# Expert dispatch: weights loaded in 1 KB runs on the ScalarE queue and put in tile order by VectorE block transposes

## The chip, the cores and the metric

The kernel runs on one core of a Trainium2 chip. The metric is the device time of one execution in microseconds (us). A profile of one execution shows what each engine and each DMA queue did; its span is a little shorter than the time, since the time also holds what lies around the program.

## What is computed

Each of 16 x 1024 tokens has a row of 512 floats and k = 2 weights, one for each of its experts. The output holds each token's row twice, each copy scaled by one weight:

```python
x_expanded = x[:, :, np.newaxis, :].repeat(k, axis=2)
weights = expert_weights[..., np.newaxis]
return (x_expanded * weights).astype(np.float32)
```

The expert indices are not used. 33.6 MB of x are read, 131 KB of weights, and 67.1 MB are written.

## The kernel before

The 16,384 tokens are cut into 8 tiles of 2,048 tokens. Partition p of a tile holds 16 consecutive tokens, so a tile of x is 128 partitions by 8,192 floats (4 MB), and each partition's part is one run of 32 KB in HBM. The weights lie in one SBUF tile of 128 x 256 floats, `w_tile`; column `c = i * 32 + t * 2 + kk` of partition p is weight kk of token t of that partition in tile i. A column of `w_tile` is thus the per-partition scalar of one multiply.

In HBM the 32 weights that a partition needs for one tile are one run of 128 B, and the runs of its 8 tiles lie 16 KB apart. L54 and L55 load them with eight DMAs on SyncE's queue, one for each tile: each has 128 rows of 128 B, 16 KB. They are issued at the start, ahead of all output.

Loads of x are issued by ScalarE (L76), one DMA per tile, into a pool of two buffers. The first two are issued at the start (L79 and L80); load i + 2 is issued at the end of tile i's loop (L109), and waits until both engines are done with the tile that had its buffer.

For each of the 16 tokens t of a tile there are two multiplies of 128 x 512: VectorE makes the copy for kk = 0 (L97, TENSOR_SCALAR) and ScalarE that for kk = 1 (L91, ACTIVATE). Eight tokens fill one `o_tile` (128 x 8,192 floats, 4 MB), of which there are four buffers. SyncE writes it to HBM (L105), so there are 16 writes, two for each tile. The multiplies of a half tile wait for its x tile, for the weights of its columns, and for an `o_tile` buffer to be written out.

[...] The scheduler places semaphore waits by region: a multiply waits for the DMA that wrote its columns of `w_tile`. It has eight semaphores for DMAs and gives them out in turn. With eight weight DMAs ahead, the second load of x got the semaphore of the first weight DMA and waits for it to land, and the eighth weight DMA got that of the first load of x and waits for that. ScalarE also loads its table of functions once (ACT_TABLE_LOAD) ahead of its first multiply.

Of the kernel before, what the change touches and what calls it, by code (L numbers as in the profile page):

```python
# [1 line left out]

# [4 lines left out]


@with_exitstack
def kernel(  # L10
    ctx: ExitStack,
    tc: tile.TileContext,
    x: bass.AP,
    expert_indices: bass.AP,
    expert_weights: bass.AP,
    out: bass.AP,
):
    nc = tc.nc

    batch, seq, hidden = x.shape  # L20
    k = expert_weights.shape[-1]
    P = nc.NUM_PARTITIONS
    ntok = batch * seq
    assert ntok % P == 0
    A_TOTAL = ntok // P

    f32 = mybir.dt.float32
    row = k * hidden
    TX = 16
    TO = 8  # L30


    groups = [[16], [16], [16], [16], [16], [16], [16], [16]]
    assert sum(sum(g) for g in groups) == A_TOTAL

    xf = x.rearrange("b s h -> (b s) h")
    of = out.rearrange("b s k h -> (b s) (k h)")
    wf = expert_weights.rearrange("b s k -> (b s) k")

    w_pool = ctx.enter_context(tc.tile_pool(name="w_pool", bufs=1))  # L40
    x_pool = ctx.enter_context(tc.tile_pool(name="x_pool", bufs=2))
    o_pool = ctx.enter_context(tc.tile_pool(name="o_pool", bufs=4))

    w_tile = w_pool.tile([P, A_TOTAL * k], f32)

    def rows(of_all, done, T):
        return of_all[done * P : (done + T) * P, :].rearrange(
            "(p a) n -> p (a n)", a=T
        )

    weights = []
    for group in groups:
        weights.append((sum(n for _, n in weights), sum(group)))
    for at, T in weights:  # L54
        nc.sync.dma_start(out=w_tile[:, at * k : (at + T) * k], in_=rows(wf, at, T))  # L55

    tiles = []
    done = 0
    for group in groups:
        T = sum(group)  # L60
        a0 = 0
        for n in group:
            tiles.append((done, T, a0, n))
            a0 += n
        done += T

    loaded = []

    def load(i):
        if i >= len(tiles):  # L70
            return
        done, T, a0, n = tiles[i]
        x_tile = x_pool.tile([P, TX * hidden], f32)
        cols = rows(xf, done, T)[:, a0 * hidden : (a0 + n) * hidden]
        for lo, hi in [(0, P)]:
            nc.scalar.dma_start(out=x_tile[lo:hi, : n * hidden], in_=cols[lo:hi, :])  # L76
        loaded.append(x_tile)

    for i in range(2):  # L79
        load(i)  # L80
    for i, (done, T, a0, n) in enumerate(tiles):
        x_tile = loaded[i]
        outr = rows(of, done, T)
        for t in range(n):
            if t % TO == 0:
                o_tile = o_pool.tile([P, TO * row], f32)
            for kk in range(k):
                c = (done + a0 + t) * k + kk
                o = t % TO * row + kk * hidden
                if kk == 1:  # L90
                    nc.scalar.mul(  # L91
                        out=o_tile[:, o : o + hidden],
                        in_=x_tile[:, t * hidden : (t + 1) * hidden],
                        mul=w_tile[:, c : c + 1],
                    )
                    continue
                nc.vector.tensor_scalar(  # L97
                    out=o_tile[:, o : o + hidden],
                    in0=x_tile[:, t * hidden : (t + 1) * hidden],
                    scalar1=w_tile[:, c : c + 1],  # L100
                    scalar2=None,
                    op0=mybir.AluOpType.mult,
                )
            if (t + 1) % TO == 0:
                nc.sync.dma_start(  # L105
                    out=outr[:, (a0 + t + 1 - TO) * row : (a0 + t + 1) * row],
                    in_=o_tile,
                )
        load(i + 2)  # L109

# [1 line left out]
_INS = ['x', 'expert_indices', 'expert_weights']  # L112
_OUTS = [((16, 1024, 2, 512), 'float32')]


# [23 lines left out]
```

## Time and profile before

| | |
|---|---|
| time, median of 3 runs | 240.91 us (240.27 to 241.28) |
| time of the profiled execution | 240.2 us |
| TENSOR_SCALAR 128 x 512, VectorE | 128 of them, mean 480 ns |
| ACTIVATE 128 x 512, ScalarE | 128 of them, mean 708 ns |
| VectorE, ScalarE busy | 51.9 us, 81.3 us |
| HBM read, written | 33.69 MB, 67.11 MB |
| rate over 0 to 10, 10 to 20, 20 to 24 us | 346, 441, 286 GB/s |
| rate over 24 to 28, 28 to 228, 228 to 238 us | 402, 433, 357 GB/s |
| issue to landing, median: x, weights, output | 23.2, 21.1, 48.3 us |

The rates come from the view of stretches, which counts a packet's bytes where it starts. The two engines that compute are idle most of the time, and what ended most of their idle time is the landing of writes (`out_dram<-o_tile`: 115.6 us of VectorE's idle time, 96.1 us of ScalarE's). A DMA's landing is when its last byte is reported; the time from issue to landing holds the time it queued.

### The profile page before, as it was taken

The page shows a single profiled execution, that of the slowest core. Times are in us where ns is not written, and L with a number is a line of the kernel's source. Part 1 is how long each engine was busy: PE and PEld are TensorE (multiplying, and loading weights), DVE is VectorE, ACT ScalarE, POOL GpSimd, SP SyncE. Part 2 cuts the span into 40 slices and gives each one's busy share as a digit, 9 for nine tenths or more (in the row PEclk, how much of TensorE's full clock was granted, in tenths as well). Part 3 has the DMA queues.
Part 4 walks back from the last instruction along what each step waited for, and adds up shares of the span by engine and source line. Part 5 has one row for each costly group of instructions (what it writes and reads, how often), then busy time and mean ns, then how long its engine had stood idle before and what let it go on. Part 6 is the DMA issues. An engine that isn't in the chain of part 4 may idle for free.

```text
span 238.4 us, 384 instructions
## 1 busy us (share of the span) xinstructions
DVE 51.9 (22%) x128; ACT 81.3 (34%) x129; POOL 0.2 (0%) x4
## 2 busy tenths in 40 slices
DVE  0072910055005004050230503204040235000000
ACT  0278970086207007080260803417043256200000
POOL 0000000000000000000000000000000000000000
DMA  7999999999999999999999999999999999999996
GB/s 266 441 442 357 441 429 412 423 429 429 440 440 440 437 434 434 440 440 418 423 429 423 434 440 440 434 440 434 440 429 440 434 429 412 429 429 440 440 440 264
DMA packets 4610, 100.81 MB, mean 423 GB/s; under 512 B 1536, under 2 KB 1536, under 8 KB 1536
## 3 DMA queue, kind: packets, MB, share of 16 engines
q1 hardware_dynamic: 3456, 67.24, 65.6%
q10 hardware_dynamic: 1152, 33.55, 33.2%
q14 instruction: 2, 0.02, 0.0%
HBM read 33.69 MB, written 67.11 MB: 423 GB/s over the span
## 4 chain that ended last, share of the span: by engine, by line
DMA 60%; another core or an unknown queue 12%; ACT 12%; ACTq 1%; issue 0%
DMA out_dram<-o_tile 41%; DMA x_tile<-in_x_dram 16%; ACT o_tile L91 12%; DMA w_tile<-in_expert_weights_dram 3%; ACTq L76 0%; ACTq L134 0%; ACTq L91 0%
## 5 line engine op out<-in xcount | busy, mean ns | idle before, releaser
L91 ACT ACTIVATE o_tile<-x_tile,w_tile 128x512 f32<-128x512 f32 x128 | 80.1, 708 | 113.9 <-DMA out_dram<-o_tile 96.1
L97 DVE TENSOR_SCALAR o_tile<-x_tile,w_tile 128x512 f32<-128x512 f32 x128 | 51.9, 480 | 150.4 <-DMA out_dram<-o_tile 115.6
L91 ACT ACT_TABLE_LOAD x1 | 1.3, 1283 | 8.7 <-DMA w_tile<-in_expert_weights_dram 8.7
L123 POOL MEMSET const-bfloat16-1.0<- 128x1 bf16 x1 | 0.1, 101 | 0.0
L123 POOL MEMSET const-uint8-127<- 128x1 uint8 x1 | 0.1, 101 | 0.0
L123 POOL MEMSET const-float32-0.0<- 128x1 f32 x1 | 0.1, 98 | 0.2 <-issue 0.2
L123 POOL MEMSET const-float32-1.0<- 128x1 f32 x1 | 0.1, 98 | 0.0
## 6 DMA issues: line engine op xcount, KB each, us to landing
out_dram<-o_tile SPq DMA_DIRECT2D x16, 4096.0 KB, 48.3
x_tile<-in_x_dram ACTq DMA_DIRECT2D x8, 4096.0 KB, 23.2
w_tile<-in_expert_weights_dram SPq DMA_DIRECT2D x8, 16.0 KB, 21.1
```

Of the source, the lines that this page charges most:

```text
L91: nc.scalar.mul(out=o_tile[:, o : o + hidden], in_=x_tile[:, t * hidden : (t + 1) * hidden], mul=w_tile[:, c : c + 1],)
L97: nc.vector.tensor_scalar(out=o_tile[:, o : o + hidden], in0=x_tile[:, t * hidden : (t + 1) * hidden], scalar1=w_tile[:, c : c + 1], scala ...
L123: nc = _bacc.Bacc("TRN2", target_bir_lowering=False, num_devices=1)
```

## The change

The eight weight DMAs on SyncE are gone. In their place ScalarE's queue gets one DMA between the loads of the first two x tiles. It reads the weights as 128 consecutive runs of 256 floats, 1 KB each, into `w_in`. In that order partition p of `w_in` holds the weights of 128 consecutive tokens, which belong to eight different partitions of one tile. VectorE brings them into the order of `w_tile`: one transpose of 32 x 32 blocks over the whole 128 x 256 (`w_mid`), and 16 transposes of 32 x 64 that gather columns of `w_mid` with a step of 32 floats and move them from one group of 32 partitions (src) to another (dst). The purpose is to replace 1,024 pieces of 128 B by 128 pieces of 1 KB, and to keep SyncE's queue for the output.

```diff
-    w_tile = w_pool.tile([P, A_TOTAL * k], f32)
...
-    for at, T in weights:
-        nc.sync.dma_start(out=w_tile[:, at * k : (at + T) * k], in_=rows(wf, at, T))
...
-    for i in range(2):
-        load(i)
+    load(0)
+    w_in = w_pool.tile([P, R * C], f32)
+    w_mid = w_pool.tile([P, R * C], f32)
+    w_tile = w_pool.tile([P, G * C], f32)
+    nc.scalar.dma_start(out=w_in, in_=wf.rearrange("(p n) -> p n", p=P))
+    nc.vector.transpose(out=w_mid, in_=w_in)
+    GQ = G // (P // B)
+    for dst in range(P // B):
+        for src in range(P // B):
+            nc.vector.transpose(
+                out=w_tile[
+                    dst * B : (dst + 1) * B, src * GQ * C : (src + 1) * GQ * C
+                ],
+                in_=w_mid[src * B : (src + 1) * B, :].rearrange(
+                    "c (q g h j) -> c g h j q", q=R, g=GQ, h=P // B
+                )[:, :, dst],
+            )
+    load(1)
```

Here P = 128, B = 32, R = 8, G = 8, C = 32 and GQ = 2. The rest of the diff rewrites the loops over tiles without changing what they issue. The transposes with src = s fill the columns of tiles 2s and 2s + 1. With the loops in this order the columns of the first two tiles are complete after the 13th small transpose (dst = 3, src = 0), and the multiplies of ScalarE wait for that one; those of VectorE stand behind all sixteen in its row. No DMA at the start shares a semaphore with another any more: the loads of x and the weights are issued without a wait. ScalarE's table load, which before waited for the first weight DMA, now waits for the first load of x.

More of the change, by code (lines that the diff above doesn't have):

```diff
@@ L30 @@
     TO = 8
-    groups = [[16], [16], [16], [16], [16], [16], [16], [16]]
-    assert sum(sum(g) for g in groups) == A_TOTAL
+    G = A_TOTAL // TX
+    C = TX * k
+    B = 32
+    R = 8
+    assert A_TOTAL % TX == 0 and C == B and G * (P // B) == B and A_TOTAL * k == R * B
     xf = x.rearrange("b s h -> (b s) h")
     of = out.rearrange("b s k h -> (b s) (k h)")
-    wf = expert_weights.rearrange("b s k -> (b s) k")
+    wf = expert_weights.rearrange("b s k -> (b s k)")
     w_pool = ctx.enter_context(tc.tile_pool(name="w_pool", bufs=1))
@@ L42, with rows @@
     o_pool = ctx.enter_context(tc.tile_pool(name="o_pool", bufs=4))
-    w_tile = w_pool.tile([P, A_TOTAL * k], f32)
-    def rows(of_all, done, T):
-        return of_all[done * P : (done + T) * P, :].rearrange(
-            "(p a) n -> p (a n)", a=T
-        )
-    weights = []
-    for group in groups:
-        weights.append((sum(n for _, n in weights), sum(group)))
-    for at, T in weights:
-        nc.sync.dma_start(out=w_tile[:, at * k : (at + T) * k], in_=rows(wf, at, T))
[L57 to L65, printed above, removed]
+    def rows(of_all, g):
+        return of_all[g * P * TX : (g + 1) * P * TX, :].rearrange(
+            "(p a) n -> p (a n)", a=TX
+        )
     loaded = []
     def load(i):
-        if i >= len(tiles):
+        if i >= G:
             return
-        done, T, a0, n = tiles[i]
         x_tile = x_pool.tile([P, TX * hidden], f32)
-        cols = rows(xf, done, T)[:, a0 * hidden : (a0 + n) * hidden]
-        for lo, hi in [(0, P)]:
-            nc.scalar.dma_start(out=x_tile[lo:hi, : n * hidden], in_=cols[lo:hi, :])
+        nc.scalar.dma_start(out=x_tile, in_=rows(xf, i))
         loaded.append(x_tile)
-    for i in range(2):
-        load(i)
-    for i, (done, T, a0, n) in enumerate(tiles):
+    load(0)
[16 more added lines that the diff above has]
+    load(1)
+    for i in range(G):
         x_tile = loaded[i]
-        outr = rows(of, done, T)
-        for t in range(n):
+        for t in range(TX):
             if t % TO == 0:
@@ L87 @@
             for kk in range(k):
-                c = (done + a0 + t) * k + kk
+                c = i * C + t * k + kk
                 o = t % TO * row + kk * hidden
@@ L95 @@
                     )
[L96 to L103, printed above, removed]
+                else:
+                    nc.vector.tensor_scalar(
+                        out=o_tile[:, o : o + hidden],
+                        in0=x_tile[:, t * hidden : (t + 1) * hidden],
+                        scalar1=w_tile[:, c : c + 1],
+                        scalar2=None,
+                        op0=mybir.AluOpType.mult,
+                    )
             if (t + 1) % TO == 0:
                 nc.sync.dma_start(
-                    out=outr[:, (a0 + t + 1 - TO) * row : (a0 + t + 1) * row],
+                    out=rows(of, i)[:, (t + 1 - TO) * row : (t + 1) * row],
                     in_=o_tile,
```

## The prediction

> **What bounds the kernel now.** I read the page first, then the chain of waits, then DMA stretches of 1 us around the chain's early steps.
>
> From the page, the span, the rate of the 40 slices, and the queues:
>
> ```profile
> span 238.4 us, 384 instructions
> DMA  7999999999999999999999999999999999999996
> GB/s 266 441 442 357 441 429 412 423 429 429 440 440 440 437 434 434 440 440 418 423 429 423 434 440 440 434 440 434 440 429 440 434 429 412 429 429 440 440 440 264
> ...
> q1 hardware_dynamic: 3456, 67.24, 65.6%
> q10 hardware_dynamic: 1152, 33.55, 33.2%
> ```
>
> The DMA engines are full in every slice but the ends and the fourth (357 GB/s, about 18 to 24 us); q1 is SyncE's queue, q10 ScalarE's. VectorE is busy 22% and ScalarE 34% of the span, so neither bounds the whole. The stretch from 28 to 228 us moves 433 GB/s (windows view). At that rate 100.81 MB take 232.8 us, so only 5.6 us of 238.4 can be had at all: a start, an end, and holes. The change touches the start and one hole.
>
> The chain of waits in order of time (start, us, what) says what the start waits for:
>
> ```profile
> 0.73 7.56 DMA w_tile<-in_expert_weights_dram
> 8.29 0.02 issue
> 8.31 15.71 DMA x_tile<-in_x_dram
> ```
>
> The second x load (L76) is issued only when the first weight DMA has landed (8.29), since they share a semaphore. It costs nothing: the first x load keeps the engines busy until 13. It lands at 24.02.
>
> The windows view (stretch, its length, DVE, ACT, POOL, clock, DMA share, GB/s) shows the fourth slice closer:
>
> ```profile
> 19.00:20.00 1.00, 0.61 (x2) 1.00 (x3) 0.00 (x0) 1.00 1.17 493
> 20.00:21.00 1.00, 0.00 (x0) 1.00 (x3) 0.00 (x0) 1.00 1.45 362
> 21.00:22.00 1.00, 0.00 (x0) 1.00 (x3) 0.00 (x0) 1.00 0.80 197
> 22.00:23.00 1.00, 0.00 (x0) 1.00 (x2) 0.00 (x0) 1.00 0.02 3
> 23.00:24.00 1.00, 0.00 (x0) 0.10 (x1) 0.00 (x0) 1.00 1.75 580
> 24.00:25.00 1.00, 0.95 (x3) 0.95 (x2) 0.00 (x0) 1.00 1.15 493
> ```
>
> Bytes count where their packet starts. Both x tiles (8.39 MB) have started by 22 (19 us at 414 from 1 to 20, plus 362 and 197 KB: 8.42 MB). A large packet lasts 33.2% of 238.4 us times 16 engines over 1024, 1.24 us, so they could end near 22.3. But large packets run again only in 23 to 24. From 18 to 28 us the mean is 377 GB/s: 10 us times (433 - 377)/433, **a hole of 1.3 us**. Yet the first write had been issued long before, by the timeline:
>
> ```profile
> 13.19 9.91 ACT L91 ACTIVATE o_tile<-x_tile,w_tile 128x512 f32<-128x512 f32 x16 [3.23 <-DMA x_tile<-in_x_dram]
> 13.19 6.42 DVE L97 TENSOR_SCALAR o_tile<-x_tile,w_tile 128x512 f32<-128x512 f32 x16 [13.19 <-DMA x_tile<-in_x_dram]
> 18.23 11.22 SPq L105 DMA_DIRECT2D out_dram<-o_tile  x3
> ```
>
> In between lie weight packets on the write's own queue: the landing of the eight weight DMAs is 7.6 at least, 21.1 median, 22.6 us at most, so most land just in the hole. The 1024 packets of 128 B are worth 0.13 MB, but their hole holds up the writes.
>
> [...]
>
> **The change, part by part.**
>
> Removed: eight weight DMAs on SyncE, 1024 packets of 128 B, and the semaphore waits between them and x loads. That frees the hole of 1.3 us, and the writes stand first on an empty queue. Added on ScalarE's queue: one load of 128 rows of 1 KB behind the first x load, and the second x load behind that, all without a wait. 131 KB at 433 GB/s are 0.3 us; I take 0.4. It delays the second x tile, whose end goes from 22.3 to about 22.4, after deducting 0.2 to 0.3 us for small packets no longer mixed in. ScalarE's table load (1.28 us) now waits for x's first tile; it ends near 14.3, hidden behind the transposes.
>
> The added wait: before, both engines multiplied from 13.19. Now VectorE first waits for the weights behind the whole first x tile: 13.0 plus 0.4, 13.4. Queued behind that wait on VectorE are all transposes and multiplies; ScalarE's first multiply waits for the 13th small transpose (the first 13 cover the columns of tiles 0 and 1), then SyncE's first write waits for eight multiplies.
>
> Price of a transpose: [...] The case's nearest row, TENSOR_SCALAR at 480 ns for 512 elements, [...] back to back it takes 6.42/16, 401 ns. [...] Estimates, all of them; no row shows a transpose.
>
> Sum: 13.4 + 0.45 + 0.1 (two semaphore steps) + 13 x 0.29 (3.8) = 17.75 for ScalarE's first multiply, 4.5 us later than before. Eight multiplies as before (18.23 - 13.19 = 5.04): first write issued at 22.8. Its packets start about 1.0 us later (first x load: issued 0.72, packets from 1 to 2 us) and, cold, may cost up to 0.9 more: the stretch from 1 to 20 us at 414 instead of 433 lost 0.8. So full flow from 23.8 to 24.7; take 24.2. Before it was about 23.6. The old hole is gone and a new one, from 22.4 to 24.2, stands in its place: **+0.6 us**. After that nothing changes: each 4 MB write takes 9.7 us at 433 and each half tile 5.0 us of ScalarE, so the queue never runs dry again; the second wave of x loads slides by 4 us behind writes that are under way. The remaining three small transposes lie behind ScalarE's longer row. 240.9 + 0.6 = 241.5.
>
> **The rivals.**
>
> *The hole closes (faster).* If the small transposes overlap at 0.14 to 0.17 us, ScalarE starts at 13.95 + 2.0 = 16.0, the write is issued at 21.0 and is there at 22.0 to 22.9, about when x's second tile ends at 22.4. The gain is bounded by the old hole: 1.3 minus the rest, 1.0 to 1.3 us: 239.7. For it: VectorE instructions of before overlap by 80 ns (480 against 401). [...]
>
> *The transposes become the bound (slower).* At 0.45 us each, or with the weights landing 1 us late since the small rows stretch the end of the first x tile as they do at 20 to 23 us: 13.4 + 0.55 + 5.85 = 19.8, write issued at 24.8, flow at 26.2: +2.6 us, 243.5. For it: nothing but transposes lies between the weights and the first write, so each 0.1 us a transpose is 1.3 us of time; the small weight rows did stretch an x tile's end. Against it: one 8 KB share per engine is far less than the packets before.
>
> *Nothing but the bytes counts (no change).* If the start is covered anyway, the time stays 240.9. The hole in the windows view speaks against it, since both versions have the engines idle there for computable times; it falls within the forecast's numbers.
>
> **How the numbers follow.** Forecast 0.5, hole closed 0.22, transposes bound 0.22, no change 0.06. The forecast itself spreads by the start of the write (0.45 us either way) and 0.04 us of a transpose (0.5): 240.5 to 242.5. Half of the closed hole passes -0.5% (239.7): faster 0.14. The bound case and a quarter of the forecast's upper part pass 242.1: slower 0.33. Same 0.53. The range is 239.5 (old hole wholly saved) to 243.4.
>
> **What would show it.** A row of 32x64 transposes near 290 ns and start to start no shorter; the weights landing near 13.4; ScalarE's first multiply near 17.8 and the first write's issue near 22.8; a stretch of about 1.5 us without bytes between 22.4 and 24.2, and the flow after it at 433. It is wrong if the transposes run at half or twice that price, if the weights land late, or if a second hole appears after 30 us.

## The result and the profile after

The changed kernel takes 242.15 us (median; 242.07 to 242.26) where the kernel before took 240.59 us beside it (240.13 to 241.28). The ratio is 1.0063, with a 95% interval of 1.0035 to 1.0091: slower by 1.6 us. The forecast was 241.5 with a range of 239.5 to 243.4, so the time lies inside the range, 0.65 us above the point. Most of the steps came out to a few tenths of a microsecond. Two did not: the hole at the start, and the sentence that nothing changes after it.

The kernel before scatters by more than the steps in question: of 193 executions beside the experiments below, 52 lie above 240.9 us, and the medians of the sets are 240.15 to 240.26. So the change may cost nearer 1.9 us than 1.6. A few executions of the variants below were in a slower state (one of e1, three of e6, one of e12), and their times below are the medians of the others.

From the page of the changed kernel, the span, the rate of the 40 slices and the rows of the transposes:

```profile
span 240.3 us, 393 instructions
GB/s 262 436 458 349 436 344 355 436 436 436 438 436 431 438 431 425 436 436 425 431 436 431 431 436 436 431 436 431 436 436 420 425 436 436 436 436 436 436 436 262
L75 DVE STREAM_TRANSPOSE w_tile<-w_mid 32x64 f32<-32x64 f32 x16 | 4.4, 275 | 0.3
L71 DVE STREAM_TRANSPOSE w_mid<-w_in 128x256 f32<-128x256 f32 x1 | 0.4, 445 | 13.2 <-DMA w_in<-in_expert_weights_dram 13.2
```

The fourth slice is low as before (349, before 357). New are the sixth and seventh, 30 to 42 us: 344 and 355, before 429 and 412. From there on the two rows differ little.

The timeline of the changed kernel (start, length, engine, line, what; in brackets the idle time ahead and what ended it) shows the added chain:

```profile
12.93 1.28 ACT L93 ACT_TABLE_LOAD   x1 [12.93 <-DMA x_tile<-in_x_dram]
13.21 0.45 DVE L71 STREAM_TRANSPOSE w_mid<-w_in 128x256 f32<-128x256 f32 x1 [13.21 <-DMA w_in<-in_expert_weights_dram]
13.69 4.63 DVE L75 STREAM_TRANSPOSE w_tile<-w_mid 32x64 f32<-32x64 f32 x16
17.46 10.52 ACT L93 ACTIVATE o_tile<-x_tile,w_tile 128x512 f32<-128x512 f32 x17 [3.24 <-DVE w_tile L75]
18.33 12.76 DVE L99 TENSOR_SCALAR o_tile<-x_tile,w_tile 128x512 f32<-128x512 f32 x32
22.49 15.03 SPq L107 DMA_DIRECT2D out_dram<-o_tile  x4
27.40 0.37 ACTq L58 DMA_DIRECT2D x_tile<-in_x_dram  x1
```

The weights land at 13.21, the sixteen small transposes take 4.63 us, 0.29 us from start to start, ScalarE starts at 17.46, when the thirteenth of them is done, and the first write is issued at 22.49. The third load of x follows at 27.40.

Stretches of 1 us of the changed kernel (length, DVE, ACT, POOL, clock, DMA share, GB/s) show the hole:

```profile
20.00:21.00 1.00, 1.00 (x4) 1.00 (x3) 0.00 (x0) 1.00 0.61 262
21.00:22.00 1.00, 1.00 (x4) 1.00 (x3) 0.00 (x0) 1.00 0.91 393
22.00:23.00 1.00, 1.00 (x3) 1.00 (x3) 0.00 (x0) 1.00 0.01 0
23.00:24.00 1.00, 1.00 (x4) 1.00 (x3) 0.00 (x0) 1.00 1.22 524
```

No packet of x or of the output starts from 22 to 23, and the writes are at full flow in 23 to 24, 0.9 us after their issue. So the new hole is no longer than the old one, although its cause is another.

Longer stretches, first of the kernel before, then of the changed one:

```profile
28.00:42.00 14.00, 2.47 (x7) 5.99 (x10) 0.00 (x0) 1.00 1.03 445
42.00:228.00 186.00, 39.08 (x96) 60.21 (x96) 0.00 (x0) 1.00 1.00 432
20.00:44.00 24.00, 6.42 (x16) 13.04 (x22) 0.00 (x0) 1.00 0.99 401
```

```profile
20.00:44.00 24.00, 11.10 (x29) 17.16 (x29) 0.00 (x0) 1.00 0.95 373
28.00:42.00 14.00, 3.10 (x8) 9.16 (x15) 0.00 (x0) 1.00 1.01 374
42.00:228.00 186.00, 39.01 (x96) 60.11 (x96) 0.00 (x0) 1.00 1.00 433
```

From 20 to 44 us the changed kernel moves (401 - 373) x 24/433, 1.55 us worth of bytes, less. After 42 us the rates agree. The difference arises there, and by this view in 28 to 42 us (445 against 374 GB/s), where both kernels have writes and loads waiting in their queues.

This view counts a packet where it starts, so a short stretch can be off by a row of 16 packets. For the comparison of all runs I use the packets of the trace themselves. In the steady part a packet of 32 KB lasts 1.213 us on one of 16 DMA engines. **Lost time** in a stretch is its length less the packets' work in it (a packet counts 1.213 us over 16, the part of it that falls in the stretch; a 16 KB packet of e9 counts half). The **even end** is where the engines would end if they shared what is left at 220 us evenly; the last end is that of the slowest engine. All in us; small negative values are the measure's own error:

| kernel | 0 to 20 | 20 to 28 | 28 to 42 | 42 to 220 | even end | last end |
|---|---|---|---|---|---|---|
| before | 2.79 | 1.42 | -0.03 | -0.27 | 236.7 | 237.3 |
| changed | 2.91 | 1.16 | 2.06 | -0.28 | 238.7 | 239.1 |
| e1, weights first | 3.13 | 0.22 | 0.53 | 0.08 | 236.8 | 237.8 |
| e2, third load later in the row | 2.86 | 1.19 | 1.80 | -0.27 | 238.4 | 239.0 |
| e3, e1 and e2 | 3.12 | 0.09 | 0.65 | -0.10 | 236.6 | 238.5 |
| e4, four transposes ahead | 2.93 | -0.01 | 0.56 | -0.10 | 236.2 | 236.9 |
| e5, third load held | 2.88 | 1.39 | 1.34 | 0.32 | 238.8 | 240.3 |
| e6, e4 and e5 | 2.86 | 0.11 | 0.33 | 1.39 | 237.5 | 239.2 |
| e7, before, weights by GpSimd | 3.01 | 0.34 | 0.74 | 0.40 | 237.3 | 239.5 |
| e8, before, first write late | 2.80 | 0.96 | 1.85 | -0.28 | 238.2 | 238.5 |
| e9, first write in two pieces | 2.98 | 0.01 | 0.85 | 0.82 | 237.5 | 238.2 |
| e10, e4 and three multiplies moved | 2.90 | 0.55 | 0.06 | 0.01 | 236.4 | 238.6 |
| e11, e4 and the load held by 0.7 us | 2.97 | -0.01 | 0.70 | -0.24 | 236.3 | 237.3 |
| e12, e10 and e11 | 2.94 | 0.43 | 0.06 | 0.41 | 236.7 | 237.9 |

Between the two kernels: 0.12 at the start, -0.26 in the hole, **+2.09 from 28 to 42 us**; the last end moves by 1.8 us and the span by 1.9. A row of this table is one execution. For most kernels it lies within 0.5 us of the median; that of e5 took 243.28 and that of e7 242.53, over 1 us more than their medians, and that of e9 241.22, 0.8 us less.

### The profile page after: what moved, and what is told of

Same layout as the page of the kernel before. It is cut to its first block, busy times and chain, and to the rows that moved or that the text cites. A ratio compares the mean times of both kernels' runs of the same rounds, so it can differ in the third digit from the quotient of the medians.

```text
span 240.3 us, 393 instructions
## 1 busy us (share of the span) xinstructions
DVE 56.6 (24%) x145; ACT 81.1 (34%) x129; POOL 0.2 (0%) x4
## 4 chain that ended last, share of the span: by engine, by line
DMA 54%; ACT 16%; another core or an unknown queue 12%; DVE 2%; ACTq 1%; issue 1%
DMA out_dram<-o_tile 39%; ACT o_tile L93 16%; DMA x_tile<-in_x_dram 11%; DMA w_in<-in_expert_weights_dram 5%; DVE w_tile L75 1%; ACTq L58 1%; ACTq L136 0%; DVE w_mid L71 0%; ACTq L93 0%
## 5 line engine op out<-in xcount | busy, mean ns | idle before, releaser
L75 DVE STREAM_TRANSPOSE w_tile<-w_mid 32x64 f32<-32x64 f32 x16 | 4.4, 275 | 0.3
```

The lines of the kernel that those rows point to most:

```text
L75: nc.vector.transpose(out=w_tile[dst * B : (dst + 1) * B, src * GQ * C : (src + 1) * GQ * C], in_=w_mid[src * B : (src + 1) * B, :].rearrange(
```

## The experiments

The question was what the stretch from 28 to 42 us loses. Theory A: the third load of x and the second write are issued in one moment (27.40 and 27.39). Theory B: the first write comes late, on engines that have run dry. The median times of all runs, each beside the kernel before on the same chip (the ratio is not the quotient of the two medians):

| run | time, us | before beside it | ratio, 95% interval |
|---|---|---|---|
| e1 | 241.15 | 240.20 | 1.0024 (1.0004 to 1.0044) |
| e2 | 242.04 | 240.20 | 1.0050 (1.0030 to 1.0069) |
| e3 | 241.73 | 240.20 | 1.0051 (1.0032 to 1.0069) |
| e4 | 240.26 | 240.20 | 0.9987 (0.9973 to 1.0000) |
| e5 | 242.25 | 240.26 | 1.0074 (1.0048 to 1.0099) |
| e6 | 241.75 | 240.26 | 1.0063 (1.0042 to 1.0083) |
| e7 | 241.19 | 240.26 | 1.0031 (1.0013 to 1.0050) |
| e8 | 241.47 | 240.26 | 1.0032 (1.0018 to 1.0047) |
| e9 | 242.03 | 240.24 | 1.0056 (1.0036 to 1.0077) |
| e10 | 242.06 | 240.24 | 1.0058 (1.0037 to 1.0079) |
| e11 | 240.35 | 240.19 | 0.9999 (0.9986 to 1.0012) |
| e12 | 240.98 | 240.15 | 1.0038 (1.0021 to 1.0054) |

**e1, the weights ahead of the first x tile.**

```diff
+    nc.scalar.dma_start(out=w_in, in_=wf.rearrange("(p n) -> p n", p=P))
     load(0)
-    nc.scalar.dma_start(out=w_in, in_=wf.rearrange("(p n) -> p n", p=P))
```

> The changed kernel with the weights' load issued ahead of the first x tile; nothing else moves. The transposes (4.9 us of VectorE) should now lie under the first x load, both engines multiply from about 13.4, and the first write is issued near 18.4, ahead of the end of the second x tile: no hole near 22. Theory A (the loss between 30 and 38 us comes from the third x load and the second write being issued in the same moment): they still are, near 23.4, so the loss of 2 us stays: 241.2. Theory B (that loss comes from the writes starting on idle engines): gone, 239.3.

The transposes run from 2.9 to 8.0 us, under the first load. VectorE multiplies from 13.58; ScalarE only from 14.84, because its table load of 1.28 us waits for the first x tile (13.55). The first write is issued at 19.88. The hole shrinks from 1.16 to 0.22 us and the later loss from 2.06 to 0.53, though the third load and the second write still coincide (24.78 and 24.77). That speaks against A. The time, 241.15, is what A gave. The profiled execution (240.74) explains part of it: the even end is back at 236.8, but the slowest engine ends 1 us behind it, where in the kernel before it is about 0.5 us.

**e2 and e3, the third load six tokens later.** In the source the load stands behind six more multiplies of ScalarE; e3 has the weights first as well.

```diff
+            if i == 1 and t == 5:
+                load(2)
...
-        load(i + 2)
+        if i > 0:
+            load(i + 2)
```

> The changed kernel with the load of the third x tile issued six tokens (3.8 us of ScalarE) later, so that it no longer coincides with the second write. The hole near 22.5 stays. Theory A: the loss after 30 us goes, about 240.1. Theory B: it stays, about 242.1.

> Both edits: weights ahead of the first x tile, third x load six tokens later. Theory A and theory B both expect neither hole nor later loss: 239.3. If it stays above 240.5, neither theory holds.

The edit did not do what it was meant to do. The timeline of e2:

```profile
27.39 0.34 SPq L109 DMA_DIRECT2D out_dram<-o_tile  x1
27.39 0.37 ACTq L58 DMA_DIRECT2D x_tile<-in_x_dram  x1
27.88 4.38 ACT L93 ACTIVATE o_tile<-x_tile,w_tile 128x512 f32<-128x512 f32 x7
```

The load is issued at 27.39 as in the changed kernel, when the sixteen multiplies it waits for are done. Either ScalarE's issuing part ran ahead of the multiplies in between, or the scheduler put the load ahead of them; the trace doesn't tell which. (That the scheduler departs from the order of the source is seen in e4 below.) So e2 repeats the changed kernel (242.04) and e3 repeats e1, at 241.73 and 241.15: two kernels that issue alike, 0.6 us apart. They say nothing on A.

**e4, the small transposes ordered by source group.** The first tiles need only the group src = 0; the others are made behind VectorE's multiplies of the first tile.

```diff
+    def spread(src):
+        for dst in range(P // B):
+            nc.vector.transpose(...)
+    spread(0)
...
+        if i == 0:
+            for src in range(1, P // B):
+                spread(src)
```

> The changed kernel with the small transposes ordered by source group, and those of later tiles behind VectorE's multiplies of the first tile: ScalarE waits for four small transposes instead of thirteen. First multiply near 14.9 instead of 17.46, first write issued near 19.9, ahead of the second x tile's end near 22.3, so no hole there. Theory A: third x load and second write still coincide: 241.2. Theory B: 239.3.

The timeline of e4:

```profile
13.90 1.44 DVE L75 STREAM_TRANSPOSE w_tile<-w_mid 32x64 f32<-32x64 f32 x5
15.07 10.52 ACT L95 ACTIVATE o_tile<-x_tile,w_tile 128x512 f32<-128x512 f32 x17 [0.65 <-DVE w_tile L75]
20.11 15.03 SPq L109 DMA_DIRECT2D out_dram<-o_tile  x4
25.01 0.37 ACTq L58 DMA_DIRECT2D x_tile<-in_x_dram  x1
```

ScalarE starts at 15.07 instead of 17.46, the first write is issued at 20.11. The row has five transposes: ScalarE starts when the fourth is done, but a fifth, which the source has behind the first tile's multiplies, stands ahead of VectorE's. The stretches of e4 at the old hole:

```profile
21.00:22.00 1.00, 0.97 (x3) 1.00 (x3) 0.00 (x0) 1.00 0.84 360
22.00:23.00 1.00, 0.93 (x5) 1.00 (x2) 0.00 (x0) 1.00 1.22 524
23.00:24.00 1.00, 0.96 (x4) 1.00 (x3) 0.00 (x0) 1.00 1.21 524
```

There is no hole at all. The loss from 28 to 42 us is 0.56. The time is 1.8 us less than that of e2, which ran beside it, and equals the kernel before. The bytes, the weights' load and the seventeen transposes are the same: what the change cost came from the thirteen small ones that stood ahead of the first write.

**e5 and e6, the third load really held.** A 128x1 multiply on ScalarE that reads the first tile's buffer after five tokens of the second tile; e5 is the changed kernel with it, e6 is e4 with it.

```diff
+            if i == 1 and t == 4:
+                nc.scalar.mul(out=mark, in_=loaded[0][:, :1], mul=w_tile[:, :1])
+                load(2)
```

> The changed kernel with the third x load really held back: a 128x1 multiply on ScalarE after five tokens of the second tile reads the first tile's buffer, so the load that takes this buffer waits for it. Issue moves from 27.4 to about 30.8, 3.4 us after the second write's. Theory A (the loss from 28 to 42 us comes from those two being issued together): loss gone, about 240.3. Theory B (the loss comes from the first write being issued late, on engines that had run dry): it stays, about 242.1. That the kernel before also issues the two 0.15 us apart (24.31 and 24.46) and loses nothing after 28 us speaks for B.

> The kernel with the small transposes ordered by source group and only four ahead of the first multiply, with the same hold of the third x load (issue from 25.0 to about 28.4). Its remaining loss from 28 to 42 us was 0.7 us. Theory A: gone, about 239.6. Theory B: stays, about 240.3.

The timeline of e5:

```profile
30.55 0.28 ACT L108 ACTIVATE mark<-x_tile,w_tile 128x1 f32<-128x1 f32 x1
30.86 0.33 ACTq L58 DMA_DIRECT2D x_tile<-in_x_dram  x1
```

The load is issued at 30.86, 3.3 us after the second write (27.61), and the time stays: 242.25. Theory A falls. By the packets the loss moved with the load: in the changed kernel the row of 16 writes that starts at 30.7 us, just ahead of the load's first packets, lasts 1.94 us in the median instead of 1.21; in e5 that row starts at 34.6 us and lasts 1.95. Holding the load where there was no hole to begin with (e6) is worse than leaving it: 241.75 against 240.26, lost in 42 to 220 us.

**e7, the kernel before with its weights issued by GpSimd.**

```diff
-        nc.sync.dma_start(out=w_tile[:, at * k : (at + T) * k], in_=rows(wf, at, T))
+        nc.gpsimd.dma_start(out=w_tile[:, at * k : (at + T) * k], in_=rows(wf, at, T))
```

> The kernel before with its eight weight DMAs issued by GpSimd instead of SyncE: same 1024 packets of 128 B, but on a queue of their own. If the old hole of 1.3 us comes from the writes standing behind them in SyncE's queue, it shrinks to below 0.5 us and the time to about 239.6. If the small packets themselves cost the engines that time, the hole stays, about 240.5.

The hole shrinks from 1.42 to 0.34 us, as the first of the two readings asked. But its page shows that the pieces are not the same:

```profile
q0 software_dynamic: 256, 0.13, 0.2%
w_tile<-in_expert_weights_dram POOLq DMA_DIRECT2D x8, 16.0 KB, 12.6
```

GpSimd's queue moves the 0.13 MB in 256 packets instead of 1024 and more (half of the 256 would be of 4 B, if each DMA has 16 of these as in the kernel before: 384 on SyncE's queue for 24 DMAs), so this run does not tell the place in the queue from the number of packets. The hoped-for 239.6 did not come: it loses 0.74 in 28 to 42, and its slowest engine ends 2.2 us behind the even end, in an execution that was 1.3 us above the median.

**e8, the kernel before with nothing changed but a later first write.** Nine VectorE instructions between the landing of the first x tile and its multiplies; the output stays the same.

```diff
+    for n in range(8):
+        nc.vector.tensor_scalar(out=zero, in0=zero if n else loaded[0][:, :hidden], scalar1=0.0, ...)
+    nc.vector.tensor_scalar(out=w_first, in0=w_tile[:, : TX * k], scalar1=zero[:, :1], ..., op0=add)
```

> The kernel before, weights and all, with nine VectorE instructions (a chain of eight on 128x512 that makes zeros out of the first x tile, and one that adds them to the first tile's weights) between the landing of the first x tile and its multiplies: the first write is issued about 4.3 us later, near 22.5, as in the changed kernel. The output is the same. Theory B: the late first write alone makes the loss, about 242. Theory A or a cause in the 1 KB load or the transposes: the old hole lasts until 23.4 anyway, so the write is not missed: about 240.8.

The timeline of e8:

```profile
13.69 3.19 DVE L84 TENSOR_SCALAR zero<-zero 128x512 f32<-128x512 f32 x7
17.20 7.46 ACT L109 ACTIVATE o_tile<-x_tile,w_first 128x512 f32<-128x512 f32 x12 [2.64 <-DVE w_first L91]
22.23 0.35 SPq L123 DMA_DIRECT2D out_dram<-o_tile  x1
```

and its stretches:

```profile
28.00:42.00 14.00, 1.96 (x5) 8.90 (x15) 0.00 (x0) 1.00 1.01 382
20.00:44.00 24.00, 9.96 (x26) 16.90 (x28) 0.00 (x0) 1.00 0.97 377
```

With no transpose and no 1 KB load in it, the kernel before shows the changed kernel's loss: 1.85 us from 28 to 42 us, where it had none, and the row of writes that starts at 30.4 us lasts 2.00 us. Theory B holds: starting the first tile's output late is enough to make the loss. (The second write and the third load come later too; e5 moved that load, and e9 below moves the first write alone.)

The hole itself even gets shorter (0.96 against 1.42), and the packets show where the old one lay. In the kernel before, the last row of the second x load lasts 2.1 us instead of 1.21, with the first write queued, and most of the 736 weight packets left at 20.7 us start only behind it, from 23.0 to 24.1. In e8, where no write is queued yet, that row lasts 1.21 us and the weight packets start from 22.0 to 23.0. So about 0.9 us of the old hole was a stretched row. Why it was stretched is open. The time rises by 1.2 us rather than the expected 1.7. The changed kernel's remaining 0.4 to 0.7 us are its longer start (2.91 against 2.80), its longer hole (1.16 against 0.96), its larger loss after it (2.06 against 1.85), and scatter between runs.

**e9, the first write in two pieces of four tokens**, otherwise the changed kernel.

```diff
+            if i == 0 and t in (3, 7):
+                nc.sync.dma_start(out=rows(of, i)[:, (t - 3) * row : (t + 1) * row], in_=o_tile[:, (t - 3) * row : (t + 1) * row])
```

> The changed kernel, transposes and all, with the first 4 MB write issued in two pieces of four tokens: the first piece is issued after four multiplies of ScalarE instead of eight, near 20.0 instead of 22.5, ahead of the second x tile's end at 22.3. Theory B (both losses, the hole near 22.5 and the slower stretch from 28 to 42 us, come from the first write being late, whatever made it late): both shrink, rate from 28 to 42 us from 374 to about 412 as in the kernel with four transposes ahead, time 240.3. If the stretch from 28 to 42 us belongs to the weights' new load or to the length of the transposes, it stays near 374 and the time near 242.

The first piece is issued at 20.17. The hole goes (0.01) and the loss from 28 to 42 falls to 0.85, with all thirteen transposes still ahead, and the second write and the third load where they were (27.47): again B, though the packets of the two pieces are 16 KB instead of 32 KB, which was not tried apart. The time does not follow: 242.03. In the profiled execution (241.22) part of the gain is lost again in 42 to 220 us (0.82), and the even end only improves to 237.5.

**e10, e11, e12: what is left.** The even end of e4 is 0.5 us ahead of that of the kernel before, but the median time is the same (its profiled execution, 239.89, was a quick one). e10 moves three of ScalarE's multiplies of the first tile to VectorE, so that the third load is issued at 23.5; e11 holds the load of e4 for one token only (25.74 instead of 25.01); e12 does both.

```diff
-                if kk == 1:
+                if kk == 1 and not (i == 0 and t in (4, 9, 14)):
```

> The kernel with only four small transposes ahead of the first multiply, and three of ScalarE's 16 multiplies of the first tile moved to VectorE: ScalarE is done with the first tile near 23.2 instead of 25.0, so the third x load and the second write are issued 1.8 us sooner, about 1.2 us after the first write's packets begin, as in the kernel before (1 us). If the remaining loss of 0.6 us from 28 to 42 us depends on how long writes ran alone before reads joined, it goes: 239.7. If not, 240.3.

> The kernel with only four small transposes ahead of the first multiply, with the third x load held for one token instead of five (128x1 multiply after the first token of the second tile): issue from 25.0 to about 25.8. In that kernel one of the 16 DMA engines took its first packet of the third x load one packet later than the other 15 and stayed out of step; the four kernels whose engines all keep one order (before, changed, e2, e8) lose nothing after 42 us, those that don't finish unevenly. Theory C (what is left is a few engines falling out of step when a load joins the writes, decided by where in the 1.21 us packet period the issue falls): with 0.8 us more all 16 take it in the same slot, the ends are even, 239.6. If the time stays at 240.3 or rises, the moment of the issue within a packet is not what decides it.

> Four small transposes ahead, three multiplies of the first tile moved to VectorE, and the third x load held for one token of the second tile (issue from 23.5 to about 24.3). The kernel with the moved multiplies alone lost 0.06 us where the third load joins the writes, but one engine fell out of step at 27.4 and ended 2 us after the others. Theory C: held by 0.8 us the engines stay in step, as in the last run, and with the smaller loss the time is 239.6, faster than both kernels. If it stays at 240.3 or more, what is saved at the start is not to be had by these moves.

e10 has next to no loss from 28 to 42 (0.06), but it loses 0.55 in 20 to 28, where e4 loses nothing, so the loss came earlier and did not go; e12 is alike (0.06 and 0.43). With an even end at 236.4 e10 still takes 242.06. The end of its profile (an execution of 241.74) shows a reason:

```profile
235.00:236.00 1.00, 0.00 (x0) 0.00 (x0) 0.00 (x0) 1.00 0.38 164
236.00:237.00 1.00, 0.00 (x0) 0.00 (x0) 0.00 (x0) 1.00 0.15 66
237.00:238.00 1.00, 0.00 (x0) 0.00 (x0) 0.00 (x0) 1.00 0.08 33
```

In 237 to 238 a single packet of 32 KB is started (33 GB/s): one DMA engine of sixteen works about two microseconds longer than most. e11 gives 240.35, with runs from 240.19 to 240.81, equal to the kernel before; there one engine took its first packet of the third load a packet early, so what was expected of theory C did not take place. In e12 all 16 engines take the third load's first packet in the same slot, as C wanted, and nothing is lost until 42 us; yet near 86 us another row of loads is stretched (0.4 us lost from 84 to 92), single engines end over 1 us behind the even end, and the time is 240.98. Theory C falls as it was put. No version here beats the kernel before; e4, at 0.9987 with an interval that reaches 1.0000, comes nearest.

## Why the prediction was right, and where it was not

**The bound, and what is to be had.** Right: the rate after 42 us is the same in both (432 and 433 GB/s), and everything happened at the start.

**The transposes.** Right to a few per cent: 275 ns of one and 0.29 us from start to start, forecast 0.29; 445 ns for the 128x256, forecast 0.45. None of the forecast's prices of a transpose (0.45 us for the large one; 0.29, 0.14 to 0.17 and 0.45 us for a small one) was worked out from a trace: no row of the kernel before shows a transpose. They were the author's estimates, so the agreement tells nothing of what a transpose's time is made up of. The small ones don't overlap: each takes 275 ns, and sixteen take 4.63 us, 0.29 us from start to start, where sixteen multiplies of VectorE, 480 ns each, take 6.42 us in the kernel before, 401 ns from start to start. The first four of e4 change only the group they write, and are 0.29 us apart too; no run here tried transposes that stay on one group, so the cause of it is not shown.

**The chain.** Right: weights at 13.21 (13.4), ScalarE's first multiply at 17.46 (17.75), first write issued at 22.49 (22.8).

**The hole.** The mechanism was right, an old hole goes and a new one comes, but the size was off: the step that let packets start 1.0 us after the issue and "cold, may cost up to 0.9 more". They started 0.9 us after it and at full rate at once, and the issue itself came 0.3 us sooner. The term of +0.6 us measured -0.26. The reading of the old hole was right in part: behind the second x tile 697 weight packets start from 23.0 to 24.1 us, and the first row of the write, issued at 18.23, only from 23.35 to 24.10; but about 0.9 us of the hole is that tile's last row, which lasts 2.1 us (e8, above).

**"After that nothing changes."** This step failed. It rested on the queue never running dry again, which is true, and took a full queue for full flow: it put the slide of the later x loads behind the writes at nothing. From 28 to 42 us the engines lost 2.06 us with writes and a load in their queues. The prediction had named a second hole after 30 us as a sign that it was wrong, and the two slow slices from 30 to 42 us are that sign, though no stretch there is without bytes. Lateness cost more here than the hole it made (1.16 us): it also changed what happened when the third load joined the writes (2.06 us). e8 shows that a late first output is enough; e4, e9 and e1 show the loss cut to 0.53 to 0.85 when the write comes sooner, with the change's own load and transposes kept. That the sum still came within 0.65 us is partly luck: one term too high by 0.9 and one left out at 2.1 would have put it 1.2 us off. Half of that went elsewhere: the kernel before ran 0.3 us quicker beside the changed one than the 240.91 that the forecast started from, and the times differ by 0.3 us less than the spans of the two profiles. Both are scatter of the kernel before, and so luck.

**The rivals.** The closed hole would have given 239.7 by the forecast. e4 closed it wholly and came to 240.3: the old hole's 1.4 us are not all to be had. By the packets of its profiled execution 0.56 comes back from 28 to 42, 0.14 at the start and 0.17 later, and its last engine ends 0.4 us sooner than in the kernel before; the medians show none of that. The transposes as the bound at 0.45 us each: no, they are at 0.29.

**What stays open.** How a late start makes a row of writes last 1.9 us instead of 1.2 when the load's first packets come, and why in most of the variants single engines drop behind later on, is not settled by these runs. What was seen: in the changed kernel, e2, e5 and e8 the 16 engines start the first write within 0.15 us of each other, and these four lose 1.34 to 2.06 us from 28 to 42. In the other ten they start it within 0.38 to 0.81 us, and none loses more than 0.85. Whether that closeness is the cause was not tried. Nor does a small loss there give a short time: of the kernels that lose under 0.9, only the kernel before, e4 and e11 come near 240.3.

## What to carry to other kernels

When a DMA-bound kernel's first output is delayed, neither the delay nor the hole it makes need be the price: here the first write came 4.3 us later, the hole at the start became 0.26 us shorter, and 2.09 us were lost where the next load joined the writes. So look for stretched packets behind the hole, with all queues full. Move from ahead of the first write all work that the first tile doesn't need: here four transposes ahead of ScalarE instead of thirteen were worth 1.8 us. Closing the hole itself brought nothing over the kernel before that the medians show (e4 240.26 beside 240.20, e11 240.35 beside 240.19): losses came back elsewhere, and in all fourteen profiles the span ends 1.1 to 1.4 us after the last packet of the slowest of 16 engines. And check in the trace when a DMA is issued: placing the load behind more multiplies in the source did not move it (e2, 27.39), while an instruction that holds its buffer did (e5, 30.86).

## What the runs showed that was not expected

- DMA engines with full queues lost about 2 us where a load joined writes that had started after a hole of about 1 us: 1.80 to 2.06 us in the changed kernel, e2 and e8, and 1.34 us in e5, against 0.3 to 0.9 where the writes followed a load with next to no gap (e1, e3, e4, e6, e7, e9, e11). e10 and e12 lost 0.06 there and 0.55 and 0.43 before it, and the kernel before none there, after a hole of 1.42.
- A write issued to idle queues flowed at full rate 0.9 us after its issue (changed kernel: issued at 22.49, 524 GB/s in 23 to 24).
- A load that stands behind 22 multiplies in the source was issued at 27.39, when only the sixteen it waited for were done. Whether ScalarE's issuing part ran ahead or the scheduler moved the load is not settled.
- Two kernels that issue alike (e1 and e3) differed by 0.6 us in their medians; the slowest DMA engine ended 0.3 to 2.2 us behind the even end, and this varied with edits that moved no bytes.
